# A decoder block on one core: linear-attention scores two heads at a time between projections, elementwise work from GpSimd to VectorE, the last modulation vector later

## Chip, cores and metric

The kernel runs on one core of one Trainium2 chip. The metric is the time of one execution on the device, in microseconds, as the median of several runs; less is better. The core has five engines with an instruction row each: TensorE (PE in the profile, with PEld for its weight loads), VectorE (DVE), ScalarE (ACT), GpSimd (POOL) and SyncE (SP), whose queue issues most transfers.

## What is computed

One decoder block over 512 tokens of width 1024 in fp32: modulation vectors from a conditioning vector, a norm, one input projection, sliding-window attention beside gated linear attention, an output projection, a second norm, and a mixture of 16384 experts of which each token takes 16 in each of 8 heads.

```python
mod = jax.nn.silu(c) @ w_ada[l] + b_ada[l]
shift1, scale1, gate1, shift2, scale2, gate2 = jnp.split(mod[:, None, :], 6, axis=-1)
h = rms_norm(x, norm1_w[l]) * (1.0 + scale1) + shift1
proj = h @ w_in[l]
aq, ak, av, gq, gk, gv, gg, glr = jnp.split(proj, split_points, axis=-1)
att = sliding_window_attention(aq, ak, av, attn_sinks[l])
log_a = jax.nn.log_sigmoid(glr @ gla_gate_up[l] + gla_gate_bias[l]) / GLA_TAU
go = gla_chunked(gq, gk, gv, log_a)
go = rms_norm(go, gla_norm_w[l]) * jax.nn.silu(gg)
x = x + gate1 * (jnp.concatenate([att, go], axis=-1) @ w_out[l])
h2 = rms_norm(x, norm2_w[l]) * (1.0 + scale2) + shift2
x = x + gate2 * peer_ffn(h2, peer_wq[l], peer_subkeys[l], peer_u[l], peer_v[l])
return rms_norm(x, final_norm_w)
```

The linear attention has 4 heads with keys of 64 and values of 128. Inside it, with b the running sum of log_a, the score of token t on token s is the sum over d of q[t,d] k[s,d] exp(b[t,d] - b[s,d]), for s up to t. The experts' part takes the 16 best keys of each half of the query, the 16 best of their 256 sums, and weighs the chosen rows of v by gelu(u . h2) times a softmax of those sums.

## The kernel before

The 512 tokens are four tiles of 128 partitions (n = 0 to 3). Every large product is made of three matmuls (`mm3`, L63): each fp32 operand is split in a high part, rounded by ScalarE (L59), and a low part, which is the subtraction source minus high part (L60) on VectorE or GpSimd.

**Front.** `mod_half` (L208) and `mod_part` (L151) make the six modulation vectors: VectorE adds eight rows of 128x1024 of w_ada, scaled (L159, L161; halves of 512 in L220 and L222), and TensorE sums over the partitions (L173, L226). `x_transposes` (L195) turns the normed x; the scaled result is split into hTh (ScalarE, L254) and hTl (GpSimd, L255). The input projection has groups of 256 columns: `proj_T` (L271) for groups 0 to 4, `proj_N` (L285) for 5 to 8 (5 and 6 the values gv, 7 and 8 the gate gg). A group's weights are split in two halves of 128x1024, the first one's low part on VectorE, the second one's on GpSimd. `attention` (L314) works two tiles of scores through softmax for each n and half of the heads.

**Linear attention.** `gla_prep` (L413) makes, for one token tile, E: nine blocks of 256 columns of differences of b (L428 on GpSimd and L429 on VectorE for seven levels, then L430, L431), the exponential of all of them (L432, ScalarE), and the products with q (L436, VectorE) and k (L437, GpSimd). `gla_scores` (L451) takes one head at a time: seven matmuls of 64 columns (L462) and two of 64x64 (L465) into one PSUM bank of tag "sc", which has two buffers, then seven predicated copies of 128x64 (L468) and two of 64x64 (L472) on VectorE, which put the scores in a triangle `at`. `gla_state` (L475) multiplies scores and values (L482) and adds what comes from the state S (L481), and renews S. `gla_gate` (L508) norms the result (gv), multiplies it with gg (L511 VectorE, L512 GpSimd) and transposes it (L515).

**Output projection and second norm.** `mixers` (L568) works two tiles n together, with w_out in halves split by GpSimd and VectorE in turn; pw is the product, mg its product with gate1 (L588, VectorE), added to x by GpSimd (L589). `second_norm` (L593) makes the statistics, xn2 (L597), its transposes x2t (L603), and h2Th and h2Tl (L608, L609); for one tile also the transposes h2n (L614).

**After that.** `wq_head` (L669) makes the queries of one of eight heads (pq; weights split by GpSimd) and their scores, of which VectorE takes the best; `u_part` (L620) makes, as a dense product, the experts' first layer for three token tiles (ph); the fourth tile's rows are gathered. Gates and second layer follow up to the end of the span.

Which instruction comes when on each engine is decided by a scheduler that simulates a timeline of the program (`TCARGS`, L38); from the routing on, VectorE's and GpSimd's rows are in the order of the code. Each engine works its row strictly in order. PSUM's front banks are in one pool, psf (L113), with tags sc (two banks), pt, po (one each) and m (two); the pool ps has two banks of tag ph. psf is closed after the routing.

Of the kernel before, what the change touches and what calls it, by code (L numbers as in the profile page):

```python
# [17 lines left out]
P = 128  # L18
# [23 lines left out]
def peer_block_kernel(ctx: ExitStack, tc: tile.TileContext, a: dict, out: bass.AP):  # L42
# [71 lines left out]
    BUFS = {"sc": 2, "pt": 1, "po": 1, "m": 2}  # L114

    def bank(name, tag="m"):
        return psf.tile([P, 512], F32, tag=tag, bufs=BUFS[tag], name=name)

# [32 lines left out]
    def mod_part(v, pool, tag, bufs, dst=None):  # L151
# [18 lines left out]
        else:  # L170
            pb = bank(f"mt{v}")
# [23 lines left out]
    def x_transposes(ks):  # L195
        for k in ks:
            pt = bank(f"xt{k}", ("sc", "sc", "pt", "po")[k % 4])
# [41 lines left out]
    for half in range(2):  # L239
# [8 lines left out]
        for k in range(4 * half, 4 * half + 4):  # L248
# [6 lines left out]
            nc.gpsimd.tensor_tensor(hTl[:, k, :], h32, hTh[:, k, :], OP.subtract)  # L255
# [15 lines left out]
    def proj_T(g, dests, new_bank=pbank):  # L271
        w = load_group(a["w_in"][g], g, 256, "wi", (nc.vector, nc.gpsimd))
# [12 lines left out]
    def proj_N(g, dst, col):  # L285
        w = load_group(a["w_in"][g], g, 256, "wi", (nc.vector, nc.gpsimd))
        for n in range(0, NT, 2):
# [26 lines left out]
    def attention(n):  # L314
# [72 lines left out]
    mod_part(2, frA, "m4", 2, gate1b)  # L387
# [25 lines left out]
    def gla_prep(n, pool):  # L413
# [10 lines left out]
        for L in range(NL):  # L424
# [3 lines left out]
            nc.gpsimd.tensor_tensor(ev[:, :, :m], ref, bv[:, :, :m], OP.subtract)  # L428
# [4 lines left out]
        for L in range(NL):  # L433
# [3 lines left out]
            nc.gpsimd.tensor_tensor(ev[:, :, :m], ev[:, :, :m], half(k, m)[:, :, :m], OP.mult)  # L437
# [9 lines left out]
    atz = [frG.tile([P, P], F32, name=f"at{i}") for i in range(8)]  # L447
# [3 lines left out]
    def gla_scores(n, q, k, E):  # L451
        U16 = mybir.dt.uint16
        for h in range(4):
            j, s = divmod(h, 2)
            r = slice(s * 64, s * 64 + 64)
            cs = slice(j * P, (j + 1) * P)
            pa = bank(f"pa{n}{h}", "sc")
            t = atz[n % 2 * 4 + h]
# [619 lines left out]
```

## Time and profile before

| | us |
|---|---|
| median of three runs | 1601.44 (1597.0 to 1605.3) |
| the profiled execution | 1596.35 |
| its span, first to last instruction | 1594.5 |
| busy: TensorE, VectorE, ScalarE, GpSimd | 1529.0, 1275.6, 677.0, 530.0 |
| granted TensorE clock, mean | 0.978 |

The profile is of one execution; its rows give durations, and its span lies 1.85 us below that execution's own time. In rows of the timeline the first number is the start in us from the span's beginning, the second the length, then engine, line, operation, result, operands, tile sizes and count; what stands in brackets is the idle time before it and the operation that ended it. Overlapping matmuls show lengths longer than their spacing; the spacing of the starts is the pace.

### The profile page before, as it was taken

Reading aid. Unit: us, or ns where it says so; the run is one execution under the profiler, and the core shown is the slowest. Engines: PE = TensorE matmul, PEld = TensorE weight load, DVE = VectorE, ACT = ScalarE, POOL = GpSimd, SP = SyncE. Lnnn points to the kernel's source line nnn. Section 1 sums busy time; section 2 is a strip of 40 time slices with the busy share of each in tenths; the row PEclk is TensorE's granted clock in tenths of the full one; section 3 lists DMA queues with packets and bytes.
Section 4 is the critical chain, followed back from the end, with each engine's and each line's share of the span. In section 5 each row is a group of like instructions: output and inputs, shape, how many; then the busy total and the mean of one; then the engine's idle time right before and its main releaser. Section 6 shows DMA issues by size and latency. Waiting matters only on the chain.

```text
span 1594.5 us, 23506 instructions
## 1 busy us (share of the span) xinstructions
PE 1529.0 (96%) x8787; PEld 1362.4 (85%) x8787; DVE 1275.6 (80%) x2588; ACT 677.0 (42%) x1073; POOL 530.0 (33%) x432
## 2 busy tenths in 40 slices
PE   4999999889999999999899999999999999999997
PEld 3768987778898999999888888888888888888885
DVE  7499887546997899798578887888888788887987
ACT  5364343653344666666233333333333333333333
POOL 3322344634430000003233343434344344343550
PEclk9999888999999999999999999999999999999998
DMA  9436522523243867679988988899989898999893
GB/s 345 146 134 239 163 75 80 185 98 105 87 167 126 252 193 245 194 223 312 412 335 316 356 330 332 336 341 354 332 333 340 329 373 322 333 342 337 285 336 132
DMA packets 154930, 409.62 MB, mean 257 GB/s; under 512 B 10288, under 2 KB 77120, under 8 KB 142400
## 3 DMA queue, kind: packets, MB, share of 16 engines
q1 hardware_dynamic: 108736, 261.30, 46.6%
q0 software_dynamic: 36864, 134.23, 22.7%
q10 hardware_dynamic: 9216, 12.59, 2.1%
q8 instruction: 69, 1.13, 0.3%
q14 instruction: 45, 0.37, 0.1%
HBM read 366.14 MB, written 41.94 MB: 256 GB/s over the span
## 4 chain that ended last, share of the span: by engine, by line
PE 61%; DVE 3%; DMA 2%; ACT 1%; issue 1%; DVEq 0%; ACTq 0%; SPq 0%
PE acc L65 11%; PE acc L64 11%; PE acc L66 11%; PE ph L66 8%; PE ph L64 8%; PE ph L65 8%; PE pg L806 4%; DMA Gd<-gs 1%; DMA gr<-Gd 1%; DVE o L799 1%; ACT gs L808 0%; DVE oh L751 0%; DVE o L794 0%; DVE oh L749 0%; DMA u<-in_uT_dram 0%
## 5 line engine op out<-in xcount | busy, mean ns | idle before, releaser
L819 POOL DMA_INDIRECT gu<-in_u_dram,ix_u x128 | 168.8, 1318 | 529.9 <-PE pg L806 273.0
L829 POOL DMA_INDIRECT gv<-in_vP_dram,ix_v x128 | 169.3, 1323 | 219.5 <-DVE gu L821 184.1
L834 DVE SCALAR_TENSOR_TENSOR gacc<-gv,hg,gacc 128x1024 f32<-128x1024 f32 x127 | 162.6, 1280 | 5.3 <-DMA gv<-in_vP_dram,ix_v 5.2
L821 DVE SCALAR_TENSOR_TENSOR gu<-gu,h2n 128x1024 f32<-128x1024 f32 x128 | 155.9, 1219 | 5.5 <-DMA gu<-in_u_dram,ix_u 5.5
L958 ACT ACTIVATE Ah<-ge 128x384 fp32r<-128x384 f32 x64 | 33.6, 525 | 157.7 <-PE acc L65 157.7
L958 ACT ACTIVATE Ah<-gel 128x384 fp32r<-128x384 f32 x64 | 33.6, 525 | 151.7 <-PE acc L65 151.7
L808 ACT ACTIVATE gs<-pg 128x512 f32<-128x512 f32 x96 | 94.0, 1110 | 8.9 <-PE pg L806 8.9
L799 DVE TENSOR_TENSOR o<-o,gp 128x1024 bf16<-128x1024 bf16 x144 | 91.0, 688 | 4.3
L806 PE MATMUL pg<-o,o 128*128 128x128 bf16 x1152 | 78.3, 222 | 5.5 <-DVE o L799 5.5
L806 PEld LDWEIGHTS <-o 128*128 128x128 bf16 x1152 | 68.8, 98 | 14.3 <-issue 7.8
L959 DVE TENSOR_TENSOR Al<-gel,Ah 128x384 fp32r<-128x384 f32 x64 | 35.6, 556 | 44.7 <-ACT Ah L958 42.1
L632 ACT ACTIVATE ge<-ph 128x384 f32<-128x384 f32 x128 | 60.7, 474 | 24.4 <-PE ph L66 24.3
L794 DVE TENSOR_TENSOR o<-iot,t 128x2048 bf16<-128x2048 bf16 x48 | 58.5, 1219 | 7.5 <-ACT t L774 7.5
L60 POOL TENSOR_TENSOR wi_1l<-wi,wi_1h 128x1024 fp32r<-128x1024 f32 x9 | 24.9, 2770 | 83.5 <-ACT wi_1h L59 83.5
L959 DVE TENSOR_TENSOR Al<-ge,Ah 128x384 fp32r<-128x384 f32 x64 | 35.5, 555 | 18.8 <-ACT Ah L958 17.6
L954 DVE TENSOR_TENSOR ge<-ge,gr 128x384 f32<-128x384 f32 x64 | 35.4, 553 | 13.0 <-ACT ge L632 13.0
L161 DVE SCALAR_TENSOR_TENSOR macc<-wa,scs,macc 128x1024 f32<-128x1024 f32 x28 | 39.3, 1403 | 2.4 <-DMA wa<-in_w_ada_dram 2.3
L468 DVE COPY_PREDICATED at<-lm,pa 128x64 f32<-128x64 uint16 x112 | 26.3, 246 | 11.5 <-PE pa L465 9.6
L700 DVE MAX8 TVa<-scm 128x8 f32<-128x128 f32 x64 | 15.1, 275 | 25.1 <-ACT scm L692 25.1
L64 PE MATMUL pq<-h2Th,wq_0h 128*128 128x512 f32 (+1 forms) x80 | 29.0, 363 | 4.8 <-ACT qha L684 2.8
L954 DVE TENSOR_TENSOR gel<-gel,gr 128x384 f32<-128x384 f32 x64 | 32.7, 552 | 0.1
L462 PEld LDWEIGHTS pa<-E 64*128 64x128 f32 x224 | 27.8, 197 | 3.2 <-issue 1.8
(2586 smaller groups left out, 5271.0 us busy)
## 6 DMA issues: line engine op xcount, KB each, us to landing
u<-in_uT_dram SPq DMA_DIRECT2D x64, 1024.0 KB
v<-in_vP_dram SPq DMA_DIRECT2D x64, 1024.0 KB
Gd<-gs SPq DMA_DIRECT2D x24, 1024.0 KB
gr<-Gd SPq DMA_DIRECT2D x16, 1536.0 KB
wa<-in_w_ada_dram SPq DMA_DIRECT2D x20, 1024.0 KB
gsp<-ge ACTq DMA_DIRECT2D x64, 192.0 KB
gel<-gsp SPq DMA_DIRECT2D x32, 384.0 KB
wi<-in_w_in_dram SPq DMA_DIRECT2D x9, 1024.0 KB
```

The source lines that it names most:

```text
L64: nc.tensor.matmul(acc, lh, rh, start=start, stop=False)
L65: nc.tensor.matmul(acc, lh, rl, start=False, stop=False)
L66: nc.tensor.matmul(acc, ll, rh, start=False, stop=stop)
L799: nc.vector.tensor_tensor(o2[:, :, m], o12[:, :, 1], gp3[:, g0:g0 + H, m, None].to_broadcast([P, H, P, 2]), OP.mult)
L806: nc.tensor.matmul(pt[:, i, :], o12[:, g, 0, :, r], o2[:, g, m, :, r], start=(m == 0), stop=(m == 2))
L808: nc.scalar.activation(gs[:, :, t0 + 4 * f:t0 + 4 * f + 4].rearrange("p b a -> p a b"), pt, AF.Copy)
L819: nc.gpsimd.indirect_dma_start(out=ur, out_offset=None, in_=a["u"], in_offset=bass.IndirectOffsetOnAxis(ap=ix_u[:, s:s + 1], axis=0))
L821: nc.vector.scalar_tensor_tensor(ur, ur, 1.0, h2n, op0=OP.mult, op1=OP.mult, accum_out=hid[:, s:s + 1])
L829: nc.gpsimd.indirect_dma_start(out=vr, out_offset=None, in_=a["vP"], in_offset=bass.IndirectOffsetOnAxis(ap=ix_v[:, s:s + 1], axis=0))
L834: nc.vector.scalar_tensor_tensor(gacc, vr, hg[:, s:s + 1], gacc, op0=OP.mult, op1=OP.add)
L954: nc.vector.tensor_tensor(ge, ge, v_part.g[:, :, c % CG, :], OP.mult)
L959: nc.vector.tensor_tensor(Al, gef, Ah, OP.subtract)
```

## The change

1. A two-bank PSUM tile (`bank2`, tag "sc2", one buffer) takes the place of the two "sc" banks. In it go pairs: two banks of x transposes, the attention scores of four heads (one VectorE operation where there were two), the linear-attention scores of two heads, the x2t transposes of tiles 0 and 2, and h2n.
2. `gla_scores` works two heads at a time: 18 matmuls in one block, and then one predicated copy for both heads where there were two (56 and 16 copies in all instead of 112 and 32). It has become a generator, one step for two heads, as is `proj_N`, with one step for half of a result; `step` lays them out in turn, and `gla_begin(3)` and the last scores come ahead of the mixers.
3. GpSimd's elementwise operations of the front go to VectorE: hTl (8), the second halves of w_in (9), the differences and products of E (28 and 28), gg times gv (4), al (8), w_out's low halves (8), x + mg (8), and the low parts of query heads 0 and 1 (4; the later heads' stay on GpSimd).
4. `mod_part(5)` moves from between projection group 8 and `gla_state(1)` to behind `wq_head(0)`, with working memory and a PSUM bank of that later stage.
5. The pool psf is closed after the mixers; a new pool psg of the same size with the same tags and with waits tile by tile serves the queries and the routing.

The core of the diff:

```diff
+    def bank2(name):
+        return psf.tile([P, 2, 512], F32, tag="sc2", bufs=1, name=name)
...
-            nc.gpsimd.tensor_tensor(hTl[:, k, :], h32, hTh[:, k, :], OP.subtract)
+            nc.vector.tensor_tensor(hTl[:, k, :], h32, hTh[:, k, :], OP.subtract)
...
-        w = load_group(a["w_in"][g], g, 256, "wi", (nc.vector, nc.gpsimd))
+        w = load_group(a["w_in"][g], g, 256, "wi", (nc.vector, nc.vector))
...
-            nc.gpsimd.tensor_tensor(ev[:, :, :m], ref, bv[:, :, :m], OP.subtract)
+            nc.vector.tensor_tensor(ev[:, :, :m], ref, bv[:, :, :m], OP.subtract)
...
     def gla_scores(n, q, k, E):
-        for h in range(4):
-            pa = bank(f"pa{n}{h}", "sc")
-            t = atz[n % 2 * 4 + h]
+        for j in range(2):
+            pa = bank2(f"pa{n}{j}")
+            t = atz[n % 2 * 2 + j]
+            for s in range(2):
+                r = slice(s * 64, s * 64 + 64)
+                for L in range(NL):
+                    nc.tensor.matmul(pa[:, s, L * 64:(L + 1) * 64], E[r, L, cs], late(E[r, L, cs], m),
+                                     start=True, stop=True)
...
-                nc.vector.copy_predicated(late(t, m), late(lm[:, L, :], m).bitcast(U16),
-                                          pa[:, L * 64:(L + 1) * 64].rearrange("p (g w) -> p g w", w=m))
+                nc.vector.copy_predicated(late2(t, m), late(lm[:, L, :], m).bitcast(U16)[:, None].to_broadcast(
+                                              [P, 2, 64 // m, m]),
+                                          pa[:, :, L * 64:(L + 1) * 64].rearrange("p a (g w) -> p a g w", w=m))
+            yield
...
+    gla_begin(0)
+    p5, p6, p7, p8 = proj_N(5, gv, 0), proj_N(6, gv, 256), proj_N(7, gg, 0), proj_N(8, gg, 256)
+    step(p5, 2)
+    step(scores[0])
+    step(p5, 3)
+    step(scores[0], 2)
+    gla_begin(1)
...
-    mod_part(5, frA, "m4", 2)
...
-                    oh, ol = hilo(wo[:, j:j + 2, :], [P, 2, 512], f"wo{n0}{q}{k4}{j}", (nc.gpsimd, nc.vector)[j // 2])
+                    oh, ol = hilo(wo[:, j:j + 2, :], [P, 2, 512], f"wo{n0}{q}{k4}{j}", nc.vector)
...
-                nc.gpsimd.tensor_tensor(x1s[i][:, qs], x1s[i][:, qs], mg, OP.add)
+                nc.vector.tensor_tensor(x1s[i][:, qs], x1s[i][:, qs], mg, OP.add)
...
-        w = load_group(a["wq"][h], h, 256, "wq", (nc.gpsimd, nc.gpsimd))
+        w = load_group(a["wq"][h], h, 256, "wq", (nc.vector, nc.vector) if h < 2 else (nc.gpsimd, nc.gpsimd))
...
     mixers(2)
     frW_s.close()
     frG_s.close()
+    fps.close()
+    bks = ExitStack()
+    banks["pool"] = bks.enter_context(tc.tile_pool(name="psg", bufs=1, space=PSUM, side="right", reuse_waits="tile"))
...
         wq_head(h)
+        if h == 0:
+            mod_part(5, gp, "gr", GR, bank("mt5", "sc"))
```

What this makes of the order, at three places. First VectorE's row behind the first copies of token tile 1's last scores: before the copies for head 3 (pa13), after those for heads 2 and 3 together (pa11). E2 is tile 2's E, wo are halves of w_out, mg00 the first output product. Before:

```order
L468 COPY_PREDICATED at7_1206<-lm_1167,pa13_1868 128x2x32
L431 COPY E2_2076<-b2_2069 128x256
L468 COPY_PREDICATED at7_1206<-lm_1167,pa13_1868 128x4x16
L418 TENSOR_SCALAR b3_2298<-la3_112 128x256
L511 TENSOR_TENSOR gg0_119<-gg0_119,gnw_82 128x512
L468 COPY_PREDICATED at7_1206<-lm_1167,pa13_1868 128x8x8
L419 SCALAR_TENSOR_TENSOR b3_2298<-sm_1192,b3_2298 128x256
L511 TENSOR_TENSOR gg1_120<-gg1_120,gnw_82 128x512
L468 COPY_PREDICATED at7_1206<-lm_1167,pa13_1868 128x16x4
L468 COPY_PREDICATED at7_1206<-lm_1167,pa13_1868 128x32x2
L468 COPY_PREDICATED at7_1206<-lm_1167,pa13_1868 128x64
L436 TENSOR_TENSOR E2_2076<-E2_2076,q2_2070 128x2x64
```

After:

```order
L442 TENSOR_TENSOR E2_1724<-E2_1724,q2_1718 128x128
L477 COPY_PREDICATED at3_1184<-lm_1149,pa11_1689 128x64x2
L443 TENSOR_TENSOR E2_1724<-E2_1724,k2_1719 128x128
L447 TENSOR_TENSOR kl2_1756<-E2_1724,k2_1719 128x256
L448 TENSOR_TENSOR qe2_1757<-E2_1724,q2_1718 128x256
L449 COPY el2_1758<-E2_1724 128x2
L60 TENSOR_TENSOR wo0100l_2400<-wo010_2397,wo0100h_2399 128x1024
L477 COPY_PREDICATED at3_1184<-lm_1149,pa11_1689 128x128
L60 TENSOR_TENSOR wo0102l_2416<-wo010_2397,wo0102h_2415 128x1024
L621 TENSOR_TENSOR mg00_2389<-pw00_2319,gate1b_84 128x512
L482 COPY_PREDICATED at3_1184<-lm_1149,pa11_1689 64x2x64 x2
```

Before, the copies from pa13's bank lie between the operations that make E2. Now they lie between the products of E2 and the low halves of w_out, and the last of them behind mg00, which needs the product pw00.

Second, TensorE's row behind the last matmuls of the output projection (pw31). Before, the queries (pq) of the first two heads follow, 71 rows of them until the transposes of tile 2:

```order
L64 MATMUL pw31_2795<-wo2142h_2848,gh3_2703 128x512
L65 MATMUL pw31_2795<-wo2142l_2849,gh3_2703 128x512
L66 MATMUL pw31_2795<-wo2142h_2848,gl3_2704 128x512
L64 MATMUL pq00_2984<-h2Th_2203,wq0_0h_2975 128x256
L65 MATMUL pq00_2984<-h2Tl_2204,wq0_0h_2975 128x256
L66 MATMUL pq00_2984<-h2Th_2203,wq0_0l_2976 128x256
```

After:

```order
L64 MATMUL pw31_2661<-wo2142h_2714,gh3_2569 128x512
L65 MATMUL pw31_2661<-wo2142l_2715,gh3_2569 128x512
L66 MATMUL pw31_2661<-wo2142h_2714,gl3_2570 128x512
L639 MATMUL x2t2_2753<-ident_73,xn2_2_2736 128x128 x8
L64 MATMUL ph0_3012<-h2Th_2191,uc0h_3008 128x384
L65 MATMUL ph0_3012<-h2Tl_2192,uc0h_3008 128x384
```

The transposes now follow at once and then the experts' product ph0; the first query matmul comes 29 rows behind the last pw31, after all transposes of tile 3 and h2n.

Third, VectorE's row at the same place, with tile 2's second norm (rb2, xn2_2). Before:

```order
L609 TENSOR_TENSOR h2Tl_2204<-h2_1_2657,h2Th_2203 128x8x128
L588 TENSOR_TENSOR mg21_2864<-pw21_2794,gate1b_84 128x512
L588 TENSOR_TENSOR mg31_2867<-pw31_2795,gate1b_84 128x512
L75 TENSOR_SCALAR rb2m_2875<-ssb2_2873 128x1
L78 TENSOR_TENSOR rb2t_2877<-rb2y_2876 128x1
L79 TENSOR_TENSOR rb2t_2877<-rb2t_2877,rb2m_2875 128x1
L80 TENSOR_SCALAR rb2t_2877<-rb2t_2877 128x1
L81 TENSOR_TENSOR rb2y_2876<-rb2y_2876,rb2t_2877 128x1
L597 TENSOR_SCALAR xn2_2_2870<-x1_2_2714,rb2y_2876 128x1024
```

After, with the modulation vector 5 (macc5, wa5), and x1 the additions that GpSimd had:

```order
L621 TENSOR_TENSOR mg31_2733<-pw31_2661,gate1b_84 128x512
L622 TENSOR_TENSOR x1_3_2582<-x1_3_2582,mg31_2733 128x512
L165 SCALAR_TENSOR_TENSOR macc5_3041<-wa5_2_3046,scs_86,macc5_3041 128x1024
L75 TENSOR_SCALAR rb2m_2741<-ssb2_2739 128x1
L165 SCALAR_TENSOR_TENSOR macc5_3041<-wa5_2_3046,scs_86,macc5_3041 128x1024
L78 TENSOR_TENSOR rb2t_2743<-rb2y_2742 128x1
L165 SCALAR_TENSOR_TENSOR macc5_3041<-wa5_4_3050,scs_86,macc5_3041 128x1024
L79 TENSOR_TENSOR rb2t_2743<-rb2t_2743,rb2m_2741 128x1
L165 SCALAR_TENSOR_TENSOR macc5_3041<-wa5_4_3050,scs_86,macc5_3041 128x1024
L80 TENSOR_SCALAR rb2t_2743<-rb2t_2743 128x1
L81 TENSOR_TENSOR rb2y_2742<-rb2y_2742,rb2t_2743 128x1
L630 TENSOR_SCALAR xn2_2_2736<-x1_2_2580,rb2y_2742 128x1024
```

One addition of x1 and four of macc5 now stand between mg31 and xn2_2; directly ahead of these rows stand two more operations of macc5, mg21 and the other addition of x1.

More of the change, by code (lines that the diff above doesn't have):

```diff
@@ L114, in peer_block_kernel @@
     BUFS = {"sc": 2, "pt": 1, "po": 1, "m": 2}
+    banks = {"pool": psf}
     def bank(name, tag="m"):
-        return psf.tile([P, 512], F32, tag=tag, bufs=BUFS[tag], name=name)
+        return banks["pool"].tile([P, 512], F32, tag=tag, bufs=BUFS[tag], name=name)
+    def bank2(name):
+        return psf.tile([P, 2, 512], F32, tag="sc2", bufs=1, name=name)
     def pbank(name):
@@ L170, in mod_part @@
         else:
-            pb = bank(f"mt{v}")
+            pb = bank(f"mt{v}") if pb is None else pb
             for i in range(KD):
@@ L196, in x_transposes @@
         for k in ks:
-            pt = bank(f"xt{k}", ("sc", "sc", "pt", "po")[k % 4])
+            if k % 4 == 0:
+                x_transposes.two = bank2(f"xt{k}")
+            pt = x_transposes.two[:, k % 4] if k % 4 < 2 else bank(f"xt{k}", ("pt", "po")[k % 2])
             for n in range(NT):
@@ L386, in peer_block_kernel @@
     proj_T(3, [[t[:, j, :] for t in gq] for j in range(2)])
-    mod_part(2, frA, "m4", 2, gate1b)
+    mod_part(2, frA, "m4", 2, dst=gate1b)
     proj_T(4, [[t[:, j, :] for t in gk] for j in range(2)])
@@ L444, in gla_prep @@
         return q, k, E, kl, qe, el
-    atz = [frG.tile([P, P], F32, name=f"at{i}") for i in range(8)]
+    atz = [frG.tile([P, 2, P], F32, name=f"at{i}") for i in range(4)]
     for t in atz:
@@ L530, in peer_block_kernel, with gla_begin, state @@
     mixd = {}
-    def gla_ahead(n):
-        prep = gla_prep(n, frG)
-        ats[n] = (gla_scores(n, *prep[:3]), *prep[3:])
-    ats = {}
-    gla_ahead(0)
-    proj_N(5, gv, 0)
-    proj_N(6, gv, 256)
-    gla_state(0, *ats[0])
-    mod_part(3, frA, "m4", 2)
-    mod_part(4, frA, "m4", 2)
-    proj_N(7, gg, 0)
-    gla_ahead(1)
-    proj_N(8, gg, 256)
-    mod_part(5, frA, "m4", 2)
-    gla_state(1, *ats[1])
-    gla_ahead(2)
+    preps, scores = {}, {}
+    def gla_begin(n):
+        preps[n] = gla_prep(n, frG)
+        scores[n] = gla_scores(n, *preps[n][:3])
+    def state(n):
+        gla_state(n, atz[n % 2 * 2:n % 2 * 2 + 2], *preps[n][3:])
+    step = lambda g, times=1: [next(g, None) for _ in range(times)]
+    gla_begin(0)
[5 more added lines that the diff above has]
+    gla_begin(1)
+    step(p6, 2)
+    step(scores[1])
+    step(p6, 3)
+    state(0)
+    mod_part(3, frA, "m4", 2)
+    step(p7)
+    step(scores[1], 2)
+    gla_begin(2)
+    step(p7, 2)
+    step(scores[2])
+    step(p7, 2)
+    mod_part(4, frA, "m4", 2)
+    state(1)
+    step(p8)
+    step(scores[2], 2)
+    gla_begin(3)
+    step(p8, 2)
+    step(scores[3])
+    step(p8, 2)
+    step(scores[3], 2)
     for t in gg:
@@ L599, in second_norm @@
         for half in range(2):
-            pt = bank(f"x2t{n}{half}", "sc").rearrange("p (a b) -> p a b", a=4)
+            if half == 0 and n % 2 == 0:
+                second_norm.two = bank2(f"x2t{n}")
+            pt = second_norm.two[:, half] if n % 2 == 0 else bank(f"x2t{n}{half}", ("pt", "po")[half])
+            pt = pt.rearrange("p (a b) -> p a b", a=4)
             for i in range(4):
@@ L610, in second_norm @@
         if n == GB:
+            two = bank2("h2n")
             for half in range(2):
-                pb = bank(f"h2n{half}", "sc")
+                pb = two[:, half]
                 for i in range(4):
```

48 lines of the change are left out of this document (22 added, 26 removed).

## Prediction

> **What bounds the kernel now.** I read the busy time by stretches first, cut at three marks of TensorE's timeline: the start of the first linear-attention score block (156.0 us), the end of the last output-projection matmul (305.1) and the start of the unbroken stretch after the second norm (337.6). Columns: window, then busy time and instructions of PE, PEld, DVE, ACT and POOL, then granted clock.
>
> ```profile
> 0.00:156.00 156.00, 131.43 (x711) 103.33 (x711) 115.98 (x241) 74.29 (x183) 47.19 (x53) 0.98 0.61 215
> 156.00:305.10 149.10, 144.58 (x892) 125.41 (x891) 120.16 (x324) 67.02 (x135) 68.80 (x68) 0.87 0.38 126
> 305.10:337.60 32.50, 22.42 (x146) 20.65 (x145) 7.75 (x16) 16.11 (x34) 12.71 (x8) 0.89 0.29 106
> 337.60:1594.00 1256.40, 1230.54 (x7041) 1112.98 (x7041) 1031.70 (x2009) 519.56 (x722) 401.26 (x304) 0.99 0.78 282
> ```
>
> TensorE is the bound in every stretch but the first 46 us and the third. Behind 337.6 it is 98% busy (1230.54 of 1256.40) and the change leaves that work as it is, so whatever moves the 337.6 us mark moves the end by as much. The question is what the front costs, and in it what TensorE loses: waits, and clock. TensorE's waits between 156 and 305 (columns: total, times, longest):
>
> ```profile
> PE gt L515 <- POOL gg L512: 1.5, 1, 1.5
> PE pw L64 <- DVE mg L588: 0.9, 1, 0.9
> PE go L481 <- DVE gv L506: 0.8, 1, 0.8
> PE pw L64 <- ACT gh L519: 0.7, 1, 0.7
> PE go L482 <- DVE at L472: 0.7, 1, 0.7
> ```
>
> They sum to 4.6 us, so in the middle it isn't waits that cost. The clock does. Two score blocks of one head back to back, in the timeline, and the clock of the ten-microsecond windows there and of two quiet neighbours:
>
> ```profile
> 220.01 1.77 PE L462 MATMUL pa<-E 64*128 64x64 f32 x14
> 221.71 0.33 PE L465 MATMUL pa<-q,k 64*64 64x64 f32 x4
> 221.97 1.77 PE L462 MATMUL pa<-E 64*128 64x64 f32 x14
> 223.67 0.33 PE L465 MATMUL pa<-q,k 64*64 64x64 f32 x4
> ...
> 210.00:220.00 10.00, 10.00 (x87) 1.00 0.00 0
> 220.00:230.00 10.00, 10.00 (x59) 0.83 0.24 66
> 280.00:290.00 10.00, 9.13 (x45) 1.00 0.79 270
> ```
>
> One head takes 1.96 us (220.01 to 221.97), two take 3.93 us, and though TensorE is busy all through, the clock falls behind such a pair. Over the middle the granted clock is 0.87, that is 2 x 0.13 x 149.1 = 39 us at half clock. The pace of the 256-wide matmuls is 0.12 us at full clock (rows 315.80 and 315.92 below) and 0.213 at half (the 202.27 and 202.49 rows are 0.22 apart), so a half-clock microsecond does 0.56 of the work:
>
> ```profile
> 202.27 0.41 PE L64 MATMUL pn<-wi_1h,hTh 128*128 128x256 f32 x1
> 202.49 0.41 PE L65 MATMUL pn<-wi_1l,hTh 128*128 128x256 f32 x1
> ```
>
> 39 x 0.44 = 17 us; I take 16, since the score matmuls themselves hardly slow down.
>
> **Start: -2.2 us.** hTl goes from GpSimd to VectorE. The rows beside each other in the timeline, first VectorE under GpSimd's hTl, then without it, and the wait it gives TensorE:
>
> ```profile
> 31.77 6.66 POOL L255 TENSOR_TENSOR hTl<-h,hTh 128x512 fp32r<-128x512 f32 x4 [2.20 <-ACT hTh L254]
> 29.89 9.09 DVE L222 SCALAR_TENSOR_TENSOR macc<-wa,scs,macc 128x512 f32<-128x512 f32 x7
> 39.41 2.33 DVE L222 SCALAR_TENSOR_TENSOR macc<-qT,scs,macc 128x512 f32<-128x512 f32 x3
> 39.03 1.26 PE L226 MATMUL mt<-ones,macc 128*128 128x1 f32 x8 [2.27 <-DVE macc L222]
> ```
>
> Seven at the quiet price are 7 x 0.78 = 5.4, so 3.7 us go; four hTl at 0.69 come to VectorE (2.8, partly ahead of these). The wait of 2.27 bounds the gain; I take 2.2, with 0 at the other end.
>
> **Middle, before any stall: -24 us.** In the new order TensorE has done 61 matmuls of the projections (44 of group 7, 17 of group 6) before the first score block that it did after it: 61 x 0.12 = 7.3. First score block at 156.0 + 7.3 - 2.2 = 161.1. From there to the last output-projection matmul TensorE has 149.1 - 4.6 (waits) - 16 (clock) - 7.3 = 121.2 us of work, so with no stall and full clock it would end at 282.3, not 305.1. Two terms come back.
>
> Clock: +4.5 us. The change fuses two heads in one block, so there are eight blocks of 3.93 us and no single ones. Before, the clock drops behind the other pairs as it does behind this one, for 3.4 us or twice that. Such a stretch costs 3.4 x 0.44 = 1.5. Four of the eight blocks, those of token tiles 0 and 1, lie where TensorE is behind and not waiting; I count three of these, 3 x 1.5 = 4.5. In the others TensorE stands anyway (next term). Ends: 0, and the present 16.
>
> The Trainium skill, page "TensorE: Matmul & The Clock Gate", section "HAM oscillation — how this bites in real kernels", ties the drop to idle gaps of more than about 3.4 us on TensorE. By that rule alone, gapless blocks cost nothing and the clock term is 0, which would take the sum 4.5 us lower. The trace disagrees: the windows above drop to 0.83 at 10.00 of 10.00 us busy. I keep the row's value.
>
> Stalls: +15 us. The scores of two heads now lie in one two-bank tile with one buffer, so a score block can't start before VectorE has copied the last of the block before. The first place is between the second block of token tile 1 and the first of tile 2. TensorE has 48 output-projection matmuls and some 20 small ones there: 48 x 0.233 + about 2 = 13 us. VectorE's row has, between the first and last copy, six lo halves, eight two-head copies, 26 E operations of 128 columns, eight of 256, three of 512 and a few small ones. Prices:
>
> ```profile
> 302.65 0.39 PE L66 MATMUL pw<-wo2142h,gl 128*128 128x512 f32 x1
> 302.88 0.40 PE L64 MATMUL pw<-wo2142h,gh 128*128 128x512 f32 x1
> ...
> 44.80 1.22 DVE L60 TENSOR_TENSOR wi_0l<-wi,wi_0h 128x1024 fp32r<-128x1024 f32 x1
> 113.22 1.48 DVE L436 TENSOR_TENSOR E<-E,q 128x128 f32<-128x128 f32 x7
> 182.93 3.48 DVE L436 TENSOR_TENSOR E<-E,q 128x128 f32<-128x128 f32 x7
> 114.61 0.42 DVE L442 TENSOR_TENSOR qe<-E,q 128x256 f32<-128x256 f32 x1
> 304.55 0.69 DVE L588 TENSOR_TENSOR mg<-pw,gate1b 128x512 f32<-128x512 f32 x1 [0.38 <-PE pw L66]
> L468 DVE COPY_PREDICATED at<-lm,pa 128x64 f32<-128x64 uint16 x112 | 26.3, 246 | 11.5 <-PE pa L465 9.6
> ```
>
> A two-head copy isn't in the trace: between 0.25 (no dearer) and 0.49 (twice one), 0.35 taken from the 0.42 - 0.21 that 128 more columns cost. E operations cost 1.48 / 7 = 0.21 with GpSimd silent; the 182.93 row is the same seven with GpSimd working beside them, and that contention goes with the change. Sum: 6 x 1.22 + 8 x 0.35 + 26 x 0.21 + 8 x 0.42 + 3 x 0.69 + 1 = 22 us, against 13: TensorE stands 9. The same happens smaller before the next three blocks, where fewer lo halves lie between copies; 6 for the three. Ends: 4.6, as before, and 32 (8 at each of four blocks). Last matmul: 282.3 + 4.5 + 15 = 301.8, or -3.3 against 305.1.
>
> What hides the rest: all of GpSimd's work of the middle (68.80 us, at VectorE's prices some 30) goes to a VectorE that had 120.16, but loses some 25 us of contention (lines 436, 429, 345 and 60), 10 of copies and 10 of the last modulation vector. It comes out at 120 + 30 - 45, about 105 of the 141 us from 161 to 302: lighter on the whole, but short of time where six lo halves stand together. ScalarE at 67 has room for four more table loads of 1.3.
>
> **Tail: +8.8 us.** Before, TensorE ran 96 matmuls of the first query heads while the second norm of token tiles 2 and 3 went on. The new pool lies over the old banks and these matmuls come behind the norm. The rows of before: last matmul, fill, first transposes, the first expert matmul, the transposes of tile 3, the mark, and the last modulation vector's price.
>
> ```profile
> 304.75 0.40 PE L66 MATMUL pw<-wo2142h,gl 128*128 128x512 f32 x1
> 305.39 0.36 PE L64 MATMUL pq<-h2Th,wq_0h 128*128 128x256 f32 x1 [0.25 <-DVE mg L588]
> 315.80 0.28 PE L64 MATMUL pq<-h2Th,wq_0h 128*128 128x256 f32 x1
> 315.92 0.28 PE L65 MATMUL pq<-h2Tl,wq_0h 128*128 128x256 f32 x1
> 316.04 0.82 PE L603 MATMUL x2t<-ident,xn 128*128 128x128 f32 x6
> 320.71 0.69 PE L64 MATMUL ph<-h2Th,uc0h 128*128 128x384 f32 x1 [3.52 <-ACT h2Th L608]
> 328.12 1.04 PE L603 MATMUL x2t<-ident,xn 128*128 128x128 f32 x8
> 337.59 0.39 PE L64 MATMUL pq<-h2Th,wq_0h 128*128 128x256 f32 x1 [2.75 <-ACT qha L684]
> 111.42 1.27 DVE L161 SCALAR_TENSOR_TENSOR macc<-wa,scs,macc 128x1024 f32<-128x1024 f32 x1
> ```
>
> With T the last matmul's end (305.1), before had x2t at T+10.9, ph at T+15.6, x2t again at T+23.0, and at T+32.5 the mark with 96 x 0.12 = 11.5 us of query work done. After, VectorE's row holds five additions of the last vector inside the chain that ends in xn: four 512-wide operations (2.8), five at 1.27 (6.4), small ones and xn (1.5), from T-0.5: x2t at T+10.2. Without the vector it would be T+3.9, so this move alone eats what VectorE gains over GpSimd's slow x additions. Then the same chain as before: ph at T+14.9, x2t at T+22.3, and 6 us for its scaling and h2n: the query matmuls begin at T+28.3 and have the 96 done at T+39.8, 7.3 us later than before; 1.5 more for the present waits for qha, which no work covers. +8.8; ends +5, and +14 if the vector's loads, which stand behind two stores on SP's queue, land late. Moving the vector takes its eight transposing matmuls out of the middle (under 2 us, inside the 121.2) and puts them in a stretch that TensorE fills. The new pool is released tile by tile and adds no other wait.
>
> **Sum.** -3.3 (which holds the start) + 8.8 = +5.5. The profiled execution took 1596.35 (span 1594.5), 5.1 below the median of the runs shown (1601.44), so that execution would become 1601.9, and the median 1606.9. I forecast 1607.
>
> **Rivals.** *VectorE keeps up.* The busy sum (105 of 141) leaves room, and if the lo halves were mostly done before the copies, the 15 us of stalls shrink to the present 4.6: -3.3 - 10.4 + 8.8 = -4.9, and without the clock loss -9.4: 1592. For it: GpSimd's contention is the largest single loss in VectorE's rows (3.48 against 1.48). Against it: the order has six lo halves between the copies, word for word.
> *The single score buffer rules.* Slower: each block of tiles 2 and 3 waits 8 us for the copies of the one before, four times, 32 instead of 15: -3.3 + 17 + 8.8 = +22.5, 1624. From 18 us of stalls on, the middle gains nothing (282.3 + 4.5 + 18 = 304.8, the present mark) and the tail's loss stands alone. For it: VectorE's load is within 16 us of TensorE's. Against: after the first place fewer lo halves lie between.
> *It does nothing that shows.* The tail's loss shrinks to 5 and the middle gains 5: 1601. For it: the tail's chain is the same length in both.
>
> **Numbers.** Forecast 0.46, VectorE keeps up 0.28, single buffer 0.16, nothing 0.10. A measurement can tell 0.5%, 8 us, from no change. The forecast's own spread (stalls 8 to 24, tail 5 to 14) is 1597 to 1618: 0.18 of it above 1609.4, 0.28 within. The first rival lies around 1592, 0.21 of it below 1593.4 and 0.07 within. So faster 0.21; same 0.28 + 0.07 + 0.10 = 0.45; slower 0.18 + 0.16 = 0.34. The range of 1588 to 1621 takes in most of the first rival and the near part of the second, and leaves out about 1 in 10 at each end.
>
> **What would show it.** Right: no GpSimd elementwise work before the last output-projection matmul, E operations at 0.21; a TensorE wait of about 9 us for the copies (line 477) before tile 2; TensorE idle for some 10 us between last pw and first x2t, with additions of line 165 before xn; the query matmuls only behind h2n. Wrong: the last pw before 292 or after 312; query matmuls in the gap; a first expert matmul under T+12; or a stretch behind the mark that isn't as long as before.

## The result, and the profile after

The changed kernel takes 1623.39 us (median of four runs, 1620.37 to 1625.71), the kernel before 1602.74 beside it: a ratio of 1.0133, 95% interval 1.0098 to 1.0168. It is slower by some 21 us, where 1607 was forecast, with 1621 as the upper end.

The two profiled executions lie further apart than the medians (spans 1594.5 and 1623.6: 29.1 us), because that of before is near its fastest run and that of after near its slowest (1625.4). Sizes in us that come from the pair are read with that in mind; sizes that come from ratios carry the verdicts.

First the stretches of the changed kernel, cut at the same events as before: first score block (159.1), last output product (314.9), and 361, where the query matmuls run. Columns as before.

```profile
159.10:314.90 155.80, 140.57 (x805) 118.96 (x804) 102.52 (x303) 66.99 (x131) 1.28 (x1) 0.84 0.26 85
...
315.00:361.00 46.00, 23.59 (x123) 21.13 (x124) 20.70 (x28) 16.41 (x35) 3.15 (x3) 0.67 0.49 170
361.00:520.00 159.00, 157.76 (x907) 145.86 (x907) 129.53 (x818) 60.51 (x85) 60.72 (x46) 1.00 0.34 121
```

The middle is 155.80 us long, 6.7 more than before, although 65 projection matmuls that came behind the first score block are now ahead of it (240 instead of 175; I had counted 61); GpSimd's column is empty (1.28); TensorE stands 15.2 us (155.80 - 140.57) and its clock is 0.84. The tail is half empty, at a clock of 0.67. Next, what TensorE waits for behind the start (columns: total, times, longest):

```profile
PE x2t L639 <- DVE xn L630: 13.7, 1, 13.7
PE pw L64 <- DVE mg L621: 7.1, 3, 3.5
...
PE ph L64 <- ACT h2Th L644: 3.5, 1, 3.5
PE pw L65 <- DVE wo0000l L60: 3.2, 1, 3.2
...
PE x2t L639 <- ACT h L642: 1.6, 1, 1.6
...
PE h2n L651 <- ACT h2n L652: 1.6, 1, 1.6
```

The longest wait is the second norm's, where the queries had been. The waits for mg and for a low half of w_out lie in the middle. None is for the copies (line 477). Two waits of 1.6 are new: the second half of x2t and of h2n waits for ScalarE's work on the first half, which lies in the same two-bank tile.

TensorE's tail in the timeline: last output product, transposes of tile 2 (two halves), first expert matmul, first query matmul.

```profile
314.59 0.40 PE L66 MATMUL pw<-wo2142h,gl 128*128 128x512 f32 x1
...
328.68 1.12 PE L639 MATMUL x2t<-ident,xn 128*128 128x128 f32 x4 [13.69 <-DVE xn L630]
...
331.39 1.11 PE L639 MATMUL x2t<-ident,xn 128*128 128x128 f32 x4 [1.59 <-ACT h L642]
...
335.99 0.69 PE L64 MATMUL ph<-h2Th,uc0h 128*128 128x384 f32 x1 [3.48 <-ACT h2Th L644]
...
349.36 0.58 PE L64 MATMUL pq<-h2Th,wq_0h 128*128 128x256 f32 x1 [0.77 <-ACT h2n L652]
```

From the last product's start, before and after: x2t at 11.3 and 14.1 us, ph at 16.0 and 21.4, the mark at 32.8 with 96 query matmuls done, and 34.8 with none. After, the 96th starts at 363.5, or 48.9, and TensorE goes on at once: the tail is 16.1 us longer. With the 9.8 by which the last product comes later (304.75 to 314.59), that is 25.9 of the 29.1 us; the other 3.2 come later. Of these, 1.8 are TensorE's own busy time behind the mark (1232.37 us from 363.5 on, against 1230.54 from 337.6 on), where the vector's matmuls now stand.

VectorE's row in the same tail, and GpSimd's one operation there:

```profile
313.62 2.68 POOL L60 TENSOR_TENSOR uc0l<-u,uc0h 128x1024 fp32r<-128x1024 f32 x1 [221.09 <-ACT uc0h L59]
...
313.98 2.86 DVE L163 TENSOR_SCALAR macc<-wa,scs 128x1024 f32<-128x1024 f32 x1
...
320.68 1.28 DVE L165 SCALAR_TENSOR_TENSOR macc<-wa,scs,macc 128x1024 f32<-128x1024 f32 x1
...
324.98 1.28 DVE L165 SCALAR_TENSOR_TENSOR macc<-wa,scs,macc 128x1024 f32<-128x1024 f32 x1 [1.63 <-DMA wa<-in_w_ada_dram]
...
327.88 0.75 DVE L630 TENSOR_SCALAR xn<-x,rb2y 128x1024 f32<-128x1024 f32 x1
```

The vector's first operation takes 2.86 us beside GpSimd, and a later one waits 1.63 for its load, with the norm's chain behind both.

In the middle, VectorE's row from the first copy of tile 1's last scores to the last, and what TensorE waits for meanwhile:

```profile
208.50 0.29 DVE L477 COPY_PREDICATED at<-lm,pa 128x128 f32<-128x128 uint16 x1
...
217.61 1.21 DVE L60 TENSOR_TENSOR wo0042l<-wo,wo0042h 128x1024 fp32r<-128x1024 f32 x1
...
227.10 0.67 DVE L621 TENSOR_TENSOR mg<-pw,gate1b 128x512 f32<-128x512 f32 x1
227.70 0.60 DVE L482 COPY_PREDICATED at<-lm,pa 64x128 f32<-64x128 uint16 x2
...
227.92 0.47 PE L64 MATMUL pw<-wo0100h,ah 128*128 128x512 f32 x1 [3.12 <-DVE mg L621]
```

19.8 us lie between the first and the last copy. TensorE does stand there, 7.3 us in all: 0.98 and 3.18 for the halves of wo0000, and 3.12 for mg, which frees the bank of the next output product, and that product stands ahead of the next scores in its row.

Last the clock: around the first score block of tile 2, in windows of ten microseconds, and the score matmuls of that block and the next:

```profile
232.40:235.80 3.40, 3.40 (x32) 3.26 (x32) 0.00 (x0) 0.00 (x0) 0.00 (x0) 1.00 0.00 0
235.90:239.20 3.30, 3.03 (x14) 2.11 (x13) 1.84 (x6) 0.85 (x5) 0.00 (x0) 0.50 0.00 0
...
240.00:250.00 10.00, 9.82 (x52) 9.03 (x53) 5.38 (x23) 0.96 (x4) 0.00 (x0) 0.50 0.00 0
...
270.00:280.00 10.00, 10.00 (x51) 8.39 (x51) 7.52 (x23) 4.02 (x13) 0.00 (x0) 0.66 0.15 60
280.00:290.00 10.00, 10.00 (x46) 8.65 (x46) 5.91 (x20) 1.07 (x4) 0.00 (x0) 0.66 0.71 254
...
232.37 1.79 PE L470 MATMUL pa<-E 64*128 64x64 f32 x14
...
241.22 3.25 PE L470 MATMUL pa<-E 64*128 64x64 f32 x14
```

For 3.4 us TensorE does nothing but score matmuls, without a gap and at full clock; then it runs at half. At half clock one head's seven 64-column matmuls, which the profile shows as fourteen rows, take 3.25 us instead of 1.79, and the whole window from 240 to 250 is at half clock.

### The profile page after: what moved, and what is told of

Same layout as the page of the kernel before. It is cut to its first block, busy times and chain, and to the rows that moved or that the text cites. A ratio compares the mean times of both kernels' runs of the same rounds, so it can differ in the third digit from the quotient of the medians.

```text
span 1623.6 us, 23358 instructions
## 1 busy us (share of the span) xinstructions
PE 1532.9 (94%) x8787; PEld 1365.0 (84%) x8787; DVE 1279.6 (79%) x2613; ACT 681.1 (42%) x1075; POOL 416.3 (26%) x323
## 3 DMA queue, kind: packets, MB, share of 16 engines
q0 software_dynamic: 36864, 134.23, 22.3%
## 4 chain that ended last, share of the span: by engine, by line
PE 58%; DVE 4%; DMA 2%; issue 1%; ACT 1%; DVEq 0%; ACTq 0%; POOLq 0%
PE acc L65 11%; PE acc L64 11%; PE acc L66 11%; PE ph L64 8%; PE ph L66 8%; PE ph L65 8%; PE pg L843 3%; DVE o L836 1%; DMA u<-in_uT_dram 1%; DMA gr<-Gd 1%; DVE o L831 1%; DMA gu<-in_u_dram,ix_u 0%; ACT gs L845 0%; DVE oh L788 0%; DVE oh L786 0%
## 5 line engine op out<-in xcount | busy, mean ns | idle before, releaser
L856 POOL DMA_INDIRECT gu<-in_u_dram,ix_u x128 | 174.6, 1364 | 532.4 <-PE pg L843 275.3
L165 DVE SCALAR_TENSOR_TENSOR macc<-wa,scs,macc 128x1024 f32<-128x1024 f32 x28 | 35.8, 1280 | 4.8 <-DMA wa<-in_w_ada_dram 4.5
L477 DVE COPY_PREDICATED at<-lm,pa 128x128 f32<-128x128 uint16 x56 | 18.9, 337 | 20.1 <-PE pa L474 19.3
L470 PE MATMUL pa<-E 64*128 64x64 f32 x224 | 33.0, 301 | 0.0
L995 DVE TENSOR_TENSOR gel<-gel,gr 128x384 f32<-128x384 f32 x64 | 32.8, 552 | 0.0
```

The source lines that it names most:

```text
L856: nc.gpsimd.indirect_dma_start(out=ur, out_offset=None, in_=a["u"], in_offset=bass.IndirectOffsetOnAxis(ap=ix_u[:, s:s + 1], axis=0))
```

## The experiments

Theory A, formed on these lines: the loss lies in the tail (no query matmuls, the modulation vector in the norm's chain) and in the clock of the middle, and VectorE with GpSimd's work is no loss. Rival B: VectorE is overloaded. Ratios are to the kernel before, with 95% intervals; the changed kernel is at 1.0133 (1.0098 to 1.0168).

| kernel | median, us | ratio | interval |
|---|---|---|---|
| ve_alone | 1607.38 | 1.0040 | 1.0011 to 1.0068 |
| mod_alone | 1606.53 | 1.0035 | 1.0008 to 1.0063 |
| two_alone | 1623.29 | 1.0160 | 1.0113 to 1.0207 |
| all_but_mod | 1614.67 | 1.0097 | 1.0059 to 1.0135 |
| fill_back | 1611.05 | 1.0069 | 1.0046 to 1.0093 |
| fill_and_mod_back | 1604.32 | 1.0023 | 1.0001 to 1.0044 |
| norm_both_halves | 1622.21 | 1.0131 | 1.0070 to 1.0193 |
| big_scores | 1585.41 | 0.9910 | 0.9870 to 0.9950 |
| before_big_scores | 1595.01 | 0.9961 | 0.9938 to 0.9985 |
| tail_on_vector | 1596.97 | 0.9979 | 0.9965 to 0.9992 |
| tail_without_htl | 1597.69 | 0.9998 | 0.9982 to 1.0014 |
| fill_mod_gp_wo | 1601.65 | 1.0005 | 0.9986 to 1.0025 |
| two_heads_and_fill | 1617.98 | 1.0111 | 1.0084 to 1.0138 |

**One part alone.** ve_alone is the kernel before with part 3 of the change:

```diff
-            nc.gpsimd.tensor_tensor(hTl[:, k, :], h32, hTh[:, k, :], OP.subtract)
+            nc.vector.tensor_tensor(hTl[:, k, :], h32, hTh[:, k, :], OP.subtract)
 (and likewise the other places of part 3)
```

> The kernel before with one part of the change alone: all of GpSimd's elementwise work of the front on VectorE. Theory A (the loss lies in the two-bank score tile with its new PSUM pool and in the modulation vector inside the second norm: an unfilled tail of some 16 us in the profiled pair, and TensorE's clock in the middle): VectorE loses its contention, the tail keeps its query matmuls, so 3 to 10 us faster than before. Theory B (VectorE is overloaded by what GpSimd gave up): 10 to 20 us slower than before, with TensorE waiting on low halves and on the gated output products in the middle.

Measured: 0.4% slower, 6 us. Both theories miss. TensorE does wait for one gated product, as theory B has it, but behind ScalarE's scaling of another tile and not behind a full VectorE; its other waits in the middle are short.

```profile
PE gt L515 <- DVE gg L512: 6.5, 1, 6.5
PE pw L64 <- DVE mg L588: 1.8, 2, 1.4
```

The gain from less contention isn't there either. The scheduler set another order of the front. Its nine executions, all in that one order, lie between 1595.9 us (granted clock 0.982) and 1609.0 (0.972), and the profile is of one at 1607.4; so the order alone doesn't give the loss, the clock goes with it, and what brings the clock down is left open.

mod_alone:

```diff
-    mod_part(5, frA, "m4", 2)
...
+        if h == 0:
+            mod_part(5, gp, "gr", GR, bank("mt5", "sc"))
```

> The kernel before with the last modulation vector alone moved behind the first query head. Theory A: the additions lie in the second norm here too, but query matmuls fill TensorE beside it, so within 5 us of before, rather slower. Theory B: no difference, since VectorE has the same work in all.

Measured: 0.35% slower, 5.6 us (1.3 to 10.1): about theory A's bound, and not theory B's nothing. TensorE waits 4.49 us for xn in front of x2t, which it did not before:

```profile
327.36 0.48 PE L602 MATMUL x2t<-ident,xn 128*128 128x128 f32 x1 [4.49 <-DVE xn L596]
```

two_alone has the parts 1, 2 and 5, with the vector's old place in the order and GpSimd's work kept:

```diff
+            pa = bank2(f"pa{n}{j}")
...
+    fps.close()
+    bks = ExitStack()
+    banks["pool"] = bks.enter_context(tc.tile_pool(name="psg", bufs=1, space=PSUM, side="right", reuse_waits="tile"))
```

> The kernel before with the two-head scores in the two-bank tile, the new order of the program and the new PSUM pool; GpSimd keeps its work and the modulation vector its place. Theory A: no query matmul between the last output product and the second transposes (9 to 12 us), and half-clock stretches behind the two-head blocks: 10 to 18 us slower than before. Theory B: VectorE isn't loaded more, so within 5 us of before.

Measured: 1.6% slower, 26 us, more than theory A's 18; the interval overlaps that of the whole change. Two-head scores with their order and their pool are the costly part, and theory B's 5 us is excluded.

**One part undone.** all_but_mod is the changed kernel with the vector back:

```diff
     step(p8, 2)
+    mod_part(5, frA, "m4", 2)
     step(scores[3], 2)
...
-        if h == 0:
-            mod_part(5, gp, "gr", GR, bank("mt5", "sc"))
```

> The changed kernel with the last modulation vector back ahead of the scores of token tile 3. Theory A: the second norm's chain loses five additions, two waits for loads and a contended first operation, 6 to 9 us, of which the middle takes back up to 5 for the same work: 2 to 9 us faster than the changed kernel. Theory B: VectorE's sum is the same, and the middle, where it is short, gets 10 us more: equal or slower than the changed kernel.

Measured: 1.0097 against 1.0133, 5.8 us less, within theory A's range; the two intervals overlap, so the size is not sure. The place where it goes can be seen: TensorE's wait for xn is 6.69 where it was 13.69, and x2t comes 7.1 us behind the last product's start (316.94) instead of 14.1.

```profile
316.94 0.40 PE L66 MATMUL pw<-wo2142h,gl 128*128 128x512 f32 x1
324.03 1.11 PE L640 MATMUL x2t<-ident,xn 128*128 128x128 f32 x4 [6.69 <-DVE xn L631]
```

fill_back opens the new pool two query heads later, so that these heads' banks are those that mg has already emptied. In the changed kernel the first query matmul waits for h2n to leave the score tile (0.77 in its row above), the last use of that tile. Whether these banks or the opening of the pool itself put the queries behind the norm, no run separates.

```diff
     frG_s.close()
-    fps.close()
-    bks = ExitStack()
-    banks["pool"] = bks.enter_context(tc.tile_pool(name="psg", ...))
...
         if h == 0:
-            mod_part(5, gp, "gr", GR, bank("mt5", "sc"))
+            mod_part(5, gp, "gr", GR, bank("mt5"))
+        if h == 1:
+            fps.close()
+            bks = ExitStack()
+            banks["pool"] = bks.enter_context(tc.tile_pool(name="psg", ...))
...
+        two = bank2(f"pss{h}") if h < 2 else None
         for n0 in range(0, NT, 2):
-            pt = bank(f"pss{h}{n0}", "sc").rearrange("p (a b c) -> p a b c", a=2, b=2)
+            pt = two[:, n0 // 2] if h < 2 else bank(f"pss{h}{n0}", "sc")
```

> The changed kernel, but the first two query heads still take their PSUM banks from the front's pool (the scores of both in a two-bank tile), and the new pool opens behind them; the order up to the last output product is the changed kernel's, row by row. 48 query matmuls then stand ahead of the second transposes of tile 2 and 34 more around the h2n transposes. Theory A (the unfilled tail is a loss of its own): those 82 matmuls at 0.12 to 0.21 us leave the path, 10 to 16 us faster than the changed kernel. Theory D (the norm's chain ends last anyway, so fill is free only in appearance): under 4 us.

Measured: 1.0069 against 1.0133, 10.2 us, at the lower end of theory A's range and outside theory D's. The intervals do not meet. TensorE's and VectorE's rows up to the last product are those of the changed kernel, operation by operation, so these 10 us come with the fill. TensorE begins the queries 3 us behind the last product, and the wait for xn is 3.54:

```profile
311.79 0.40 PE L66 MATMUL pw<-wo2142h,gl 128*128 128x512 f32 x1
314.75 0.55 PE L64 MATMUL pq<-h2Th,wq_0h 128*128 128x256 f32 x1 [2.56 <-DVE mg L621]
...
325.75 1.12 PE L639 MATMUL x2t<-ident,xn 128*128 128x128 f32 x4 [3.54 <-DVE xn L630]
```

fill_and_mod_back joins that edit and the one of all_but_mod.

> As fill_back, with the last modulation vector back ahead of the scores of tile 3 as well. Theory A: the chain is shorter by the vector's additions, but query matmuls now cover part of what they cost, so it gains less on top than the 9 us that the vector alone was worth: 13 to 20 us faster than the changed kernel, up to 8 slower than before. Theory D: as all_but_mod, 9 us faster than the changed kernel.

Measured: 1.0023, 17.6 us less than the changed kernel, as theory A had it; its interval lies just below that of fill_back, so the vector costs something of its own. The wait for xn is down to 0.6. Of the 21 us of the change, these two things hold 17.6, and 3.7 stay.

norm_both_halves takes the wait inside the two-bank tile of x2t away:

```diff
+        pts = []
         for half in range(2):
...
+            pts.append(pt)
             for i in range(4):
                 k = 4 * half + i
                 nc.tensor.transpose(pt[:, i, :], xn2[:, k * P:(k + 1) * P], ident)
+        for half in range(2):
+            pt = pts[half]
```

> The changed kernel, but the second norm issues the transposes of both halves of a token tile ahead of the evictions of either. In the changed kernel the second half of x2t waits 1.6 us for the evictions of the first, which lie in the same tile. If these waits are on the path: 1 to 3 us faster than the changed kernel. If they aren't: no difference.

Measured: 1.0131 (1.0070 to 1.0193). In its profile the wait of 1.6 in x2t is gone, but that for h2Tl is 4.5 where it was 0.8. With two runs, 1 to 3 us can't be told from nothing: left open.

**The score matmuls.** big_scores leaves the scores' true values out: one matmul for each head stands where nine were, and the copies and their dependences stay. The scheduler lays the middle out in another order, so the matmuls aren't the only thing that differs in the trace.

```diff
-                for L in range(NL):
-                    m = 64 >> L
-                    nc.tensor.matmul(pa[:, s, L * 64:(L + 1) * 64], E[r, L, cs], late(E[r, L, cs], m), ...)
-                for i in range(2):
...
+                nc.tensor.matmul(pa[:, s, :], E[r, 0, cs], E[r, 0:2, :].rearrange("p a b -> p (a b)"),
+                                 start=True, stop=True)
```

> The changed kernel with one matmul of 512 columns for each head's scores in place of nine small ones: the scores aren't the reference's, all else is done as before. It takes the small matmuls away and leaves their copies and waits. Theory A (the small matmuls in blocks of 3.9 us bring the clock down): the clock of the middle rises from 0.84 to 0.95 or more, the eight blocks shrink from 32 us to 4, and it's 30 us or more faster than the changed kernel. Theory C (the waits for VectorE bring the clock down): the clock stays under 0.90, waits grow, 8 to 18 us faster.

Measured: 0.9910 against 1.0133, 36 us faster than the changed kernel, as theory A had it, but its clock only in part. The middle, from the first score matmul to the last output product:

```profile
158.50:278.70 120.20, 103.50 (x550) 78.70 (x549) 99.66 (x297) 65.16 (x131) 1.37 (x1) 0.91 0.34 108
```

0.91 is 2 x 0.09 x 120.2 = 22 us at half clock, against 2 x 0.16 x 155.8 = 50. So 28 of the 50 go with the small matmuls, and 22 stay, beside waits of still 16.7 us (theory C's part).

before_big_scores is the same edit in the kernel before.

> The kernel before with one matmul of 512 columns for each head's scores in place of nine small ones (the scores aren't the reference's). Counterpart of big_scores, which was 38 us faster than the changed kernel. The blocks shrink by 16 x 1.7 = 27 us at full clock. If the prediction's 16 us of clock in the kernel before hang on these blocks, it's 35 to 45 us faster than before; if VectorE and GpSimd set the pace as soon as TensorE is relieved, 10 to 25, with more waits.

Measured: 6 us faster (0.4%); the expectation's first case falls, and even its second was too high. Relieved of some 27 us of matmuls, TensorE waits more. Its middle, from the first score matmul to the last output product, and the longest waits there:

```profile
168.30:309.90 141.60, 119.29 (x610) 90.46 (x608) 115.61 (x315) 63.76 (x131) 67.71 (x69) 0.90 0.39 127
...
PE gt L510 <- POOL gg L507: 4.1, 1, 4.1
PE pS L487 <- ACT kn L483: 3.6, 1, 3.6
PE mt L173 <- DVE macc L161: 3.0, 1, 3.0
PE pk L481 <- DVE S L492: 2.6, 1, 2.6
```

It stands 22.3 us in 141.6, where it stood 4.5 in 149.1: of some 27 us, 18 come back as waits, and the middle is 7.5 us shorter. (The profiled execution took 1600.36 us; its first score block comes 12 us later than in the kernel before, at 168.4.) The waits name VectorE, GpSimd and ScalarE. So in the kernel before, these engines are almost as close to being the bound as TensorE, 97% busy as that is. The same relief gave 36 us in the changed kernel, where the waits of the middle hardly rise (15.2 to 16.7): there VectorE has room.

**What the move to VectorE is worth.** two_heads_and_fill is fill_and_mod_back with GpSimd's work back on GpSimd.

> As two_alone, with the first two query heads in the front's pool, so that query matmuls stand ahead of the second transposes again: two-head scores in the two-bank tile, GpSimd keeps its work, the modulation vector its place. It is fill_and_mod_back without the move to VectorE. If the move relieves the middle (GpSimd's contention was what set VectorE's pace): 5 to 15 us slower than fill_and_mod_back, which was 0.23% over before. If the move overloads VectorE: level with it or faster.

Measured: 1.0111 against 1.0023: the move gains 0.88%, 14 us, beside two-head scores. Rival B falls. Here the wait for the score tile's copies, which the prediction had named, does appear:

```profile
PE pa L470 <- DVE at L482: 3.8, 1, 3.8
PE pw L64 <- DVE mg L622: 3.4, 2, 3.0
PE gt L526 <- POOL gg L523: 2.2, 1, 2.2
```

GpSimd is not what brings it: all_but_mod and fill_and_mod_back, with VectorE doing that work, show the same wait (3.3 us each, 3.0 the longest). All three keep the last vector in the middle, in an order of their own; the changed kernel and fill_back, which don't, show no such wait. What in the order makes it is left open.

fill_mod_gp_wo puts every second low half of w_out back on GpSimd, in fill_and_mod_back:

```diff
-                    oh, ol = hilo(wo[:, j:j + 2, :], [P, 2, 512], f"wo{n0}{q}{k4}{j}", nc.vector)
+                    oh, ol = hilo(wo[:, j:j + 2, :], [P, 2, 512], f"wo{n0}{q}{k4}{j}", (nc.gpsimd, nc.vector)[j // 2])
```

> As fill_and_mod_back, with every second low half of w_out back on GpSimd. If the waits in the middle come from the low halves standing in VectorE's row between the copies and mg: the waits before the output products shrink by the 1.2 us of each of the three halves at each place, 3 to 6 us faster than fill_and_mod_back. If GpSimd's contention costs as much: no difference or slower.

Measured: 1.0005 against 1.0023, 2.9 us, in the expected direction, with intervals that overlap. It is level with the kernel before.

tail_on_vector and tail_without_htl are the kernel before with few pieces on VectorE, the second without the first line pair:

```diff
-            nc.gpsimd.tensor_tensor(hTl[:, k, :], h32, hTh[:, k, :], OP.subtract)
+            nc.vector.tensor_tensor(hTl[:, k, :], h32, hTh[:, k, :], OP.subtract)
...
-                nc.gpsimd.tensor_tensor(x1s[i][:, qs], x1s[i][:, qs], mg, OP.add)
+                nc.vector.tensor_tensor(x1s[i][:, qs], x1s[i][:, qs], mg, OP.add)
...
-        w = load_group(a["wq"][h], h, 256, "wq", (nc.gpsimd, nc.gpsimd))
+        w = load_group(a["wq"][h], h, 256, "wq", (nc.vector, nc.vector) if h < 2 else (nc.gpsimd, nc.gpsimd))
```

> The kernel before with three of GpSimd's pieces on VectorE and nothing else: hTl, the additions of mg to x, and the low halves of query heads 0 and 1. Theory A (at the start and in the tail GpSimd's slowness and its contention lie on the path; elsewhere VectorE is better left alone): 2 us from the start, 3 to 6 us from an earlier second norm, of which the query matmuls beside it already cover part: 2 to 8 us faster than before, the only one of these kernels on that side. Rival: the second norm's chain ends under the query matmuls in any case, within 2 us of before.

Measured: 0.9979, 3.4 us faster than before: within theory A's range, and the only kernel with the true scores whose interval lies below that of no change.

> As tail_on_vector, but hTl stays on GpSimd: the kernel before with the additions of mg to x and the low halves of query heads 0 and 1 on VectorE, nothing else. In the profile of tail_on_vector TensorE waits 5.1 us for a low half of w_in that stands behind hTl in VectorE's row, and the clock falls to 0.52 behind it. If that cost is real: 3 to 8 us faster than tail_on_vector, 6 to 12 faster than before. If it's made good later: as tail_on_vector, 3 us faster than before.

Measured: 0.9998 (0.9982 to 1.0014): a miss for both cases. A faster second norm alone gains nothing that can be told from noise; that the query matmuls cover it is argued, not shown. The wait of 5.1 us in tail_on_vector is from an execution of 1606.39 us (median 1596.97), and this comparison doesn't find it in the median. The two intervals overlap, so what hTl itself is worth stays open.

## Why the prediction was wrong

The direction of the sum was right (+5.5), the size not (+21). The sum was -3.3 up to the last output product and +8.8 for the tail; by the runs that undo the tail's two losses it was about +3.7 and +17.6. By its own steps:

**Start (-2.2): held as far as can be seen.** The first score block, forecast for 161.1, began at 159.1 in the profile.

**Stalls (+15): the size held, the releaser did not.** TensorE stood 15.2 us in the middle. The 22 us of VectorE's row between first and last copy measured 19.8. At that first place TensorE stood 7.3, for the 9 forecast. But the waits are for mg and a low half, in the same row, and not for the copies. That the sum came out as forecast is partly luck. The rival of the single score buffer names 1624, which is what was measured; its mechanism isn't: four waits of 8 us for copies appear nowhere, and what makes its number is the clock and the tail.

**Clock (+4.5): mis-sized; this is the first failed step.** I counted three half-clock stretches that lose 1.5 us each. The middle's 155.8 us less 121.2 of work and 15.2 of waits leave 19.4 for the clock, and 0.84 gives 50 us at half clock, or 50 x 0.44 = 22. Two of my premises are wrong. The score matmuls do slow down (3.25 us for 1.79), so a block that starts at half clock is longer. And blocks among waits keep the clock down, up to a whole window at 0.50, where I had written "in the others TensorE stands anyway" and counted nothing.

The Trainium skill, page "TensorE: Matmul & The Clock Gate", section "HAM oscillation — how this bites in real kernels", ties the half clock to idle gaps of TensorE of more than about 3.4 us. The trace disagrees: 240 to 250 ran at 0.50 with TensorE busy for 9.82 of 10, the half clock from 235.9 on follows 3.4 us of score matmuls without a gap, and with one large matmul for each head big_scores lost 28 of the 50 us at half clock. So small matmuls go with the half clock in these runs. The other 22 stayed with the waits, of which the longest in that middle is 3.0 us; what holds the clock down there is open.

**Work of the middle (-24): a premise was wrong.** The heading's 24 isn't what the sum uses: from 305.1 to 282.3 lie 2.2 of the start, 4.6 of waits and 16 of clock, so the middle's part is 20.6. I took TensorE as the bound of the middle, from 97% busy. before_big_scores shows that VectorE, GpSimd and ScalarE stood close behind. VectorE's own load was forecast well (105 us, measured 102.52). Contention was named as the largest loss in VectorE's rows and given to a rival; the move that ends it was worth 14 us beside two-head scores (two_heads_and_fill). Without that gain, the change would have been slower still.

**Tail (+8.8): mis-sized; the second failed step.** It was 16.1 in the profiled pair, and 17.6 by the runs that undo it. The lost fill was rightly seen, and is 10.2 by fill_back. The chain was forecast to reach x2t at T+10.2, T being the end of the last product, and reached it at T+13.7: the vector's first operation, 2.86 beside GpSimd instead of the 0.74 of the same form alone, and a load that came 1.63 late, which stood only in the range. Then the second half of x2t waited for the first half's evictions (1.59), a wait of the two-bank tile that I did not see. And the 96 query matmuls took 14.1 us (349.36 to 363.5) and not 11.5, since the clock, at 0.67 over the stretch, had gone down in the empty tail.

What remains: with both tail losses undone 3.7 us are left (0.23%, 0.01 to 0.44). Without the move to VectorE it is 18 us (two_heads_and_fill), so a loss of 18 with the two-head scores and a gain of 14 largely cancel. How much of the 18 is clock, how much waits and how much the new order is not settled, nor what makes the last 1.4 us behind the mark in the profiled pair.

## What to carry to other kernels

A pool that is closed and reopened can change which work fills a gap: look for what ran there before, and price the gap without it. An engine at 97% isn't proof of a bound: take work away from it once and see what the time does. Small matmuls, short waits and the clock are not separate terms; where blocks of small matmuls stand among waits, price both at the half clock.

## What the runs showed of the hardware

- A head's seven 64-column score matmuls (fourteen rows of 64x64) take 1.77 to 1.79 us at full clock and 3.25 at half.
- The half clock comes with TensorE busy all the time too: 0.66 in two windows of 10.00 of 10 busy, and 0.50 right behind 3.4 us of score matmuls without a gap.
- A VectorE scaling of 128x1024 (line 163) took 2.86 us beside a GpSimd subtraction of that size and 0.74 alone (at 107.36), and one E operation runs at a pace of 0.20 us when GpSimd is silent, against 3.48 / 7 = 0.50 beside it. The Trainium skill, page "GPSIMD Engine Reference", section "8. Key points", says that the two engines share their ways into SBUF; these rows agree.
